# Stick-breaking attention on one core: five softplus chains issued two banks deep, and the weighted values issued at the end of the next pair's period

## The chip, the cores and the metric

One core of a Trainium2 chip runs the whole kernel in one launch. The metric is device microseconds (us) of that core. The engines spoken of are TensorE (PE: matrix products into PSUM, which has eight banks here), VectorE (DVE), ScalarE (ACT), GpSimd (POOL) and SyncE (SP, which issues the loads of the weights).

## What is computed

Two transformer blocks on one sequence of 512 tokens, 1024 wide, in float32. The change lies in the attention of the second block: sixteen heads of 64, each query weighs earlier keys by a stick that is broken key by key.

```python
def stick_breaking_attention(xn, w_qkv, q_gain, k_gain, w_o):
    qkv = (xn @ w_qkv).reshape(b, s, 3, SB_HEADS, SB_HEAD_DIM)
    q = rms_norm(qkv[:, :, 0], q_gain)       # k likewise; v plain
    ...
    z = einsum('bhqd,bhkd->bhqk', q, k) * scale
    mask = s_idx < t_idx
    log_beta = log_sigmoid(z)
    log_1m = where(mask, log_sigmoid(-z), 0.0)
    rev = cumsum(log_1m, axis=3, reverse=True)
    rev_excl = concatenate([rev[..., 1:], 0])
    w = where(mask, exp(log_beta + rev_excl), 0.0)
    outs.append(einsum('bhqk,bhkd->bhqd', w, v))
    ...
    return o @ w_o
```

With sp = softplus(z) the weight is exp(z - sp - sum of sp over the keys between), which is how the kernel forms it.

## The kernel before

**The whole.** Four feed-forward parts, a first mixer and this attention follow each other. Nearly all products are made of three matmuls each (`mm3`, lines 180 to 182): weights and activations are split into a high part, rounded to fp32r by ACT (line 157 for a weight, line 175 for an activation), and the rest, made by DVE (lines 158 and 176).

**The attention stage.** A generator, `sb_dense`, issues the projections that make Q, K and V: `qk_tile` for two heads' Q or K, `sv_tile` for a quarter of V, then part of the output projection. A second one, `stick`, issues the attention of one pair of heads after the other, eight pairs, 0 to 7. `Flow` (F) lets them take turns: after each `yield n` of `stick`, n steps of `sb_dense` are issued (`F.pull(n)`). One step is three matmuls of 512 columns, or six of 256 in `sv_tile`. `F.at(d, f)` runs f when d more steps have been issued. So a Q or K tile's norm follows its projection: `first` scales it (line 759) and squares it on ACT (line 761), and seven steps on `second` sums the squares with one matmul (line 766, into a bank `pm`), takes the inverse root on ACT (lines 209, 210) and DVE (lines 212 to 214), and scales the tile (line 769).

**One pair.** `front` (lines 833 to 842) takes five PSUM banks, A1, A0, Z2, B1 and B0, and fills them with the scores of the two heads: head A lies in A0, A1 and half of Z2, head B in B0, B1 and the other half. `soft` makes softplus of a bank in place of four operations, each on 128x512: magnitude on DVE (line 850), exponential and logarithm on ACT (lines 851, 852), and on DVE the sum with max(z, 0) (line 853). `split` makes high and low parts of the result (lines 175 and 176). `middle(.., g)` subtracts the running sums with matmuls into the same banks (lines 865 to 871): g = 0 is head A, which needs the softplus of A1, A0, Z2 and the splits of these three in that order, g = 1 is head B. `weights` takes the exponential of a bank (line 874), which is its last use. `back` (lines 878 to 885) multiplies the weights of a pair with V into a bank `po`, and splits that.

**What sets the order.** PE, ACT and SP execute in the order in which the code issues. DVE and POOL are put into an order by a scheduler when the program is built, and that order is fixed from then on. Buffers come from pools: eight banks of PSUM (`bank`), 66 slots of 128x512 (`sl`).

In the code before, a bank's four softplus operations are issued together, and the `back` of the pair before stands in the midst of the pair's period, ahead of `middle`.

Of the kernel before, what the change touches and what calls it, by code (L numbers as in the profile page):

```python
# [10 lines left out]
I32 = mybir.dt.int32  # L11
F32R = mybir.dt.float32r
AF = mybir.ActivationFunctionType
OP = mybir.AluOpType
# [60 lines left out]
def block_kernel(ctx: ExitStack, tc: tile.TileContext, a, out):  # L75
    nc = tc.nc
    dve, act, pe, pool = nc.vector, nc.scalar, nc.tensor, nc.gpsimd
# [9 lines left out]
    def sl(dt=F32):  # L87
        return slots.tile([P, S], dt, name="sl", tag="sl")

    def bank():  # L90
        return psum.tile([P, S], F32, name="ps", tag="ps")
# [236 lines left out]
    F = Flow()  # L328
# [421 lines left out]
    def qk_tile(n, which, g):  # L750
        ps = bank()
        yield from proj(ps, a["sb_qk"][n], 1024, zs)
        if "r2" not in state:
            state["r2"] = nx.rstd()
            F.at(7, lambda: column_of(state["r2"], rcol2))

        def first():
            t = sl()
            dve.tensor_tensor(t, ps, state["r2"], op=OP.mult)
            sq = sl()  # L760
            act.activation(sq, t, AF.Square)
            F.at(NORM_LAG, lambda: second(t, sq))

        def second(t, sq):
            pm = bank()
            pe.matmul(pm, halves, sq, start=True, stop=True)  # L766
            rs = sl()
            rsqrt(rs, pm, 1.0 / 64)
            dve.scalar_tensor_tensor(t, t, g, rs, op0=OP.mult, op1=OP.mult)
            if which is K:  # L770
                pool.tensor_copy(kz[n % 3][HALF[1], :], t[HALF[1], 2 * P:3 * P])
            F.at(SCALE_LAG, lambda: which.__setitem__(n % 8, t))
        F.at(1, first)
# [48 lines left out]
    def stick():  # L822
# [19 lines left out]
                    pe.matmul(z[b][:, c:c + P], ident_r, hidden_r, start=False, stop=True, skip_group_check=True)  # L842
            return z

        def soft(z):

            def one(b):
                t = sl()

                dve.tensor_scalar(t.bitcast(I32), z[b].bitcast(I32), 0x7FFFFFFF, None, op0=OP.bitwise_and)  # L850
                act.activation(t, t, AF.Exp, scale=-1.0)  # L851
                act.activation(t, t, AF.Ln, bias=1.0)  # L852
                dve.scalar_tensor_tensor(t, z[b], 0.0, t, op0=OP.max, op1=OP.add)  # L853
                return t
            return one

        def middle(z, sp, hl, g):
            for j in ((3, 1, 0, 2), (3, 1, 2, 0))[g]:
# [30 lines left out]
        for n in range(KD):  # L889
            while n not in K and F.pull(1):  # L890
                pass
            while n not in K:
                F.t += 1
                F.fire()
            z = front(n)
            one = soft(z)
            sp, hl = {}, {}
            sp[A1] = one(A1)
            yield 2
            sp[A0] = one(A0)  # L900
            yield 2
            hl[A1] = split(sp[A1])
            sp[Z2] = one(Z2)
            yield 2
            hl[A0] = split(sp[A0])
            sp[B1] = one(B1)
            yield 3
            hl[Z2] = split(sp[Z2])
            if n:
                while v[1][(n - 1) // 2] is None and F.pull(1):  # L910
                    pass
                back(n - 1, last)
            yield 2
            sp[B0] = one(B0)
            hl[B1] = split(sp[B1])
            middle(z, sp, hl, 0)
            yield 1
            hl[B0] = split(sp[B0])
            yield 3
            weights(z, sp, A1)  # L920
            weights(z, sp, A0)
            middle(z, sp, hl, 1)
            for b in (B1, Z2, B0):
                weights(z, sp, b)
            yield 5
            last = sp
        yield 7
        back(KD - 1, last)
# [1 line left out]
    F.dense = sb_dense()  # L930
    for steps in stick():
        F.pull(steps)
    while F.pull(1):
        pass
    F.settle()

    norm = Norm()
# [127 lines left out]
```

## Time and profile before

| | us |
|---|---|
| median of three runs | 2193.16 |
| lowest, highest | 2192.76, 2193.18 |
| the profiled execution | 2191.18 |
| its span (first to last instruction) | 2189.4 |
| attention stage, from the scores of pair 0 to the end of the values of pair 7 | 1509 to 1795 |
| DVE and ACT busy, share of the span | 50%, 38% |

The profile is of one execution. An engine's busy time is the time in which it executes something. "Idle before" in brackets is how long an engine stood still ahead of an instruction, with the engine, tile and line that released it. PEclk is the granted TensorE clock as a share of 2.4 GHz; 0.50 is 1.2 GHz. In a row of the timeline that stands for several matmuls, the duration is that of the whole row.

### The profile page before, as it was taken

What the parts mean: (1) busy time and instruction counts of PE and PEld (TensorE: products, weight loads), DVE (VectorE), ACT (ScalarE), POOL (GpSimd) and SP (SyncE); (2) the same over time, 40 slices, a digit from 0 to 9 for tenths busy, and PEclk for the clock granted to TensorE, in tenths of its full rate; (3) what the DMA queues carried; (4) which work ended last, traced back from release to release, by engine and by line L of the source; (5) the groups of instructions that cost most, each with busy time, mean ns of one, the idle gap of its engine ahead of it and who ended that gap; (6) DMA issues with size and microseconds to landing.
All of it is one profiled execution on the core that took longest, in us unless ns stands there. A gap on an engine that the chain in (4) does not pass through costs nothing.

```text
span 2189.4 us, 24877 instructions
## 1 busy us (share of the span) xinstructions
PE 2126.0 (97%) x10038; PEld 1747.2 (80%) x10038; DVE 1097.2 (50%) x1600; ACT 829.7 (38%) x1287; POOL 24.2 (1%) x50
## 2 busy tenths in 40 slices
PE   8999999999999999999999999998988899999999
PEld 6888888887888788888888888886766678888887
DVE  6444334799945644444454444346555646444332
ACT  5222222376766432222233222224454445222211
POOL 0000000000002000000000000000000000000000
PEclk9999999999999999999999999999999999999999
DMA  4332334222212333333323233331111113323341
GB/s 163 112 96 97 89 97 118 88 91 71 78 44 79 109 97 96 97 97 91 102 79 114 97 97 93 101 101 62 48 35 43 39 37 117 97 97 96 93 122 54
DMA packets 57267, 193.43 MB, mean 88 GB/s; under 512 B 6784, under 2 KB 6784, under 8 KB 57152
## 3 DMA queue, kind: packets, MB, share of 16 engines
q1 hardware_dynamic: 55296, 188.28, 27.3%
q0 software_dynamic: 640, 2.10, 0.3%
q8 instruction: 78, 1.28, 0.2%
q10 hardware_dynamic: 1216, 1.47, 0.2%
q14 instruction: 37, 0.30, 0.0%
HBM read 189.07 MB, written 2.10 MB: 87 GB/s over the span
## 4 chain that ended last, share of the span: by engine, by line
PE 80%; issue 9%; DVE 8%; ACT 3%; DMA 0%; POOL 0%; SPq 0%; DVEq 0%; POOLq 0%
PE ps L180 25%; PE ps L181 24%; PE ps L182 24%; DVE wl L158 1%; PE ps L883 1%; DVE sl L176 1%; ACT sl L851 1%; ACT sl L852 1%; PE ps L871 1%; DVE sl L495 1%; PE ps L870 1%; DVE sl L850 1%; PE ps L865 1%; DVE m L493 1%; PE ps L766 0%
## 5 line engine op out<-in xcount | busy, mean ns | idle before, releaser
L180 PE MATMUL ps<-sl,wh 128*128 128x512 f32 x2704 | 1069.3, 395 | 10.0 <-ACT sl L247 6.5
L181 PE MATMUL ps<-sl,wh 128*128 128x512 f32 x2704 | 1057.0, 391 | 2.4 <-DVE sl L248 1.6
L182 PE MATMUL ps<-sl,wl 128*128 128x512 f32 x2704 | 1056.0, 391 | 0.0
L180 PEld LDWEIGHTS ps<-sl,wh 128*128 128x128 f32 x2704 | 509.7, 189 | 120.5 <-issue 6.8
L181 PEld LDWEIGHTS ps<-sl,wh 128*128 128x128 f32 x2704 | 510.1, 189 | 109.2 <-issue 2.9
L182 PEld LDWEIGHTS ps<-sl,wl 128*128 128x128 f32 x2704 | 509.8, 189 | 107.3
L158 DVE TENSOR_TENSOR wl<-wraw,wh 128x1024 fp32r<-128x1024 f32 (+3 forms) x368 | 434.8, 1183 | 313.4 <-ACT wh L157 312.9
L157 ACT ACTIVATE wh<-wraw 128x1024 fp32r<-128x1024 f32 (+3 forms) x368 | 373.0, 1015 | 514.4 <-issue 238.0
L175 ACT ACTIVATE sl<-sl 128x512 fp32r<-128x512 f32 x145 | 91.0, 627 | 394.6 <-DVE sl L277 383.2
L277 DVE TENSOR_TENSOR sl<-ps,sl 128x512 f32<-128x512 f32 x88 | 60.9, 692 | 265.9 <-PE ps L182 259.9
L176 DVE TENSOR_TENSOR sl<-sl 128x512 fp32r<-128x512 f32 x145 | 101.7, 701 | 72.0 <-ACT sl L175 71.0
L275 DVE TENSOR_TENSOR sl<-ps,sl 128x512 f32<-128x512 f32 x88 | 60.8, 691 | 138.5 <-PE ps L182 138.3
L228 ACT ACTIVATE sl<-x 128x512 f32<-128x512 f32 x42 | 25.8, 627 | 123.6 <-DVE x L297 97.4
L296 DVE SCALAR_TENSOR_TENSOR sl<-ps,sl 128x512 f32<-128x512 f32 x32 | 22.1, 692 | 79.7 <-PE ps L182 79.7
L276 ACT ACTIVATE sl<-sl 128x512 f32<-128x512 f32 x88 | 54.1, 615 | 12.2 <-DVE sl L275 12.2
L883 PE MATMUL ps<-sl 128*64 128x512 f32 (+3 forms) x128 | 25.8, 551 | 32.1 <-DVE sl L213 20.5
L514 ACT ACTIVATE sl<-sl,mx 128x128 f32<-128x128 f32 (+3 forms) x64 | 35.7, 558 | 41.1 <-DVE mx L513 41.0
L851 ACT ACTIVATE sl<-sl 128x512 f32<-128x512 f32 x40 | 25.1, 628 | 66.7 <-DVE sl L850 66.7
L883 PEld LDWEIGHTS ps<-sl 128*64 128x64 f32 x128 | 10.0, 168 | 48.3 <-DVE sl L213 21.6
L853 DVE SCALAR_TENSOR_TENSOR sl<-ps,sl 128x512 f32<-128x512 f32 x40 | 27.7, 692 | 40.9 <-ACT sl L852 40.9
L521 ACT ACTIVATE sl<-sl,sm 128x128 f32<-128x128 f32 (+3 forms) x64 | 35.9, 560 | 25.3 <-DVE sm L520 14.6
L597 PE MATMUL ps<-sl 128*128 128x256 f32 (+2 forms) x176 | 43.2, 327 | 0.8 <-DVE mx L513 0.8
(136 smaller groups left out, 1333.9 us busy)
## 6 DMA issues: line engine op xcount, KB each, us to landing
wraw<-in_f_in_dram SPq DMA_DIRECT2D x176, 512.0 KB
wraw<-in_f_out_dram SPq DMA_DIRECT2D x64, 512.0 KB
wraw<-in_mix_t_dram SPq DMA_DIRECT2D x34, 512.0 KB
wraw<-in_f_out_dram SPq DMA_DIRECT2D x32, 384.0 KB
wraw<-in_sb_qk_dram SPq DMA_DIRECT2D x16, 512.0 KB
wraw<-in_br_dram SPq DMA_DIRECT2D x16, 256.0 KB
wraw<-in_w_out_dram SPq DMA_DIRECT2D x8, 512.0 KB
wraw<-in_sb_v_dram SPq DMA_DIRECT2D x8, 512.0 KB
```

The lines of the kernel that those rows point to most:

```text
L157: act.activation(wh[:, :n], raw[:, :n], AF.Copy)
L158: dve.tensor_tensor(wl[:, :n], raw[:, :n], wh[:, :n].bitcast(F32), op=OP.subtract)
L175: act.activation(h, x, AF.Copy)
L176: dve.tensor_tensor(l, x, h.bitcast(F32), op=OP.subtract)
L180: pe.matmul(ps, wh, xh, start=start, stop=False)
L181: pe.matmul(ps, wh, xl, start=False, stop=False)
L182: pe.matmul(ps, wl, xh, start=False, stop=stop)
L275: dve.tensor_tensor(g, pg, rs, op=OP.mult)
L276: act.activation(g, g, AF.Silu)
L277: dve.tensor_tensor(g, pu, g, op=OP.mult)
L851: act.activation(t, t, AF.Exp, scale=-1.0)
L883: pe.matmul(po[HALF[g], sb * P:], v[sb // 2][n // 2][:, cv:cv + 64], t[b][:, c:c + S - sb * P], start=sb == 0, stop=sb == 3)
```

## The change

The four softplus operations become three functions, and a loop of six turns issues them shifted against each other: in one turn the magnitude of the bank after next, the exponential and logarithm of this bank, the sum of the bank before, and the split of the bank before that. Each of the first four turns is followed by three steps of projections, the other two by one. `middle` of head A then comes after fourteen steps; the split of B1 is issued behind it. `back` of the pair before goes from ahead of `middle` to behind the weights of the present pair, and ahead of it further steps are issued until six have passed since the last norm matmul (`bank_free`) and until the V tile is there. Two steps then stand between `back` and the next pair's scores. At the end the rest of `sb_dense` is issued until it is exhausted. No operation is added or removed, and the loads are the same.

```diff
         def second(t, sq):
             pm = bank()
+            state["bank_free"] = F.t + 6
...
             z = front(n)
-            one = soft(z)
             sp, hl = {}, {}
-            sp[A1] = one(A1)
-            yield 2
-            sp[A0] = one(A0)
-            yield 2
-            hl[A1] = split(sp[A1])
-            sp[Z2] = one(Z2)
-            yield 2
-            hl[A0] = split(sp[A0])
-            sp[B1] = one(B1)
-            yield 3
-            hl[Z2] = split(sp[Z2])
-            if n:
-                while v[1][(n - 1) // 2] is None and F.pull(1):
-                    pass
-                back(n - 1, last)
-            yield 2
-            sp[B0] = one(B0)
+            order = (A1, A0, Z2, B1, B0)
+            for t in range(6):
+
+                for b in order[:2] if t == 0 else order[t + 1:t + 2]:
+                    sp[b] = absolute(z, b)
+                if t < 5:
+                    log_part(sp[order[t]])
+                if 1 <= t:
+                    soft(sp[order[t - 1]], z[order[t - 1]])
+                if 2 <= t < 5:
+                    hl[order[t - 2]] = split(sp[order[t - 2]])
+                yield 3 if t < 4 else 1
+            middle(z, sp, hl, 0)
             hl[B1] = split(sp[B1])
-            middle(z, sp, hl, 0)
             yield 1
             hl[B0] = split(sp[B0])
             yield 3
...
             for b in (B1, Z2, B0):
                 weights(z, sp, b)
-            yield 5
+            yield 1
+            if n:
+                while F.t < state["bank_free"] and F.pull(1):
+                    pass
+                while v[1][(n - 1) // 2] is None and F.pull(1):
+                    pass
+                back(n - 1, last)
+            yield 2
             last = sp
...
-    while F.pull(1):
-        pass
+    while F.dense is not None:
+        F.pull(1)
```

The three places below are all in the period of pair 4. Lines of the changed kernel are a little higher: the norm matmul is 767, the magnitude 849, exponential and logarithm 853 and 854, the sum 858, `middle` 868 to 874, the weights 877, `back` 886.

On PE before, from the norm matmul of a K tile into its bank ps_12401 on; ps_12427 is the bank `po` of pair 3:

```order
L766 MATMUL ps_12401<-sl_12351,cmat_102 128x512
L180 MATMUL ps_12413<-sl_10382,wh_12170 128x512
L181 MATMUL ps_12413<-sl_10383,wh_12170 128x512
L182 MATMUL ps_12413<-sl_10382,wl_12171 128x512
L883 MATMUL ps_12427<-sl_12063,sl_12108 64x512
L883 MATMUL ps_12427<-sl_12214,sl_12108 64x512
L883 MATMUL ps_12427<-sl_12046,sl_12108 64x384
```

On PE now, from the norm matmul of that tile on; ps_12265 to ps_12268 are banks of pair 4:

```order
L767 MATMUL ps_12434<-sl_12375,cmat_102 128x512
L180 MATMUL ps_12446<-sl_10382,wh_12195 128x512
L181 MATMUL ps_12446<-sl_10383,wh_12195 128x512
L182 MATMUL ps_12446<-sl_10382,wl_12196 128x512
L868 MATMUL ps_12267<-sl_12325,nlater_11064 128x128
L868 MATMUL ps_12266<-sl_12325,nones_11066 128x128
L868 MATMUL ps_12267<-sl_12325,nones_11066 128x128
L868 MATMUL ps_12268<-sl_12325,nones_11066 128x128
L873 MATMUL ps_12267<-sl_12413,nlater_r_11068 128x384
```

Before, one step and then `back` followed the norm matmul; now one step and then `middle` of head B does, and `back` comes after five more steps.

On ACT before, from the split of A1 on; sl_12338, 12356, 12371, 12386 and 12446 are the softplus tiles of A1, A0, Z2, B1 and B0, and sl_12419 is a projected tile on the way to its norm:

```order
L175 ACTIVATE sl_12367<-sl_12338 128x512
L851 ACTIVATE sl_12371<-sl_12371 128x512
L852 ACTIVATE sl_12371<-sl_12371 128x512
L175 ACTIVATE sl_12382<-sl_12356 128x512
L851 ACTIVATE sl_12386<-sl_12386 128x512
L852 ACTIVATE sl_12386<-sl_12386 128x512
L157 ACTIVATE wh_12397<-wraw_12175 128x1024
L209 ACTIVATE sl_12404<-ps_12401,epst_105 128x512
L210 ACTIVATE sl_12404<-sl_12404 128x512
L761 ACTIVATE sl_12421<-sl_12419 128x512
L175 ACTIVATE sl_12423<-sl_12371 128x512
L175 ACTIVATE sl_12436<-ps_12427 128x512
```

On ACT now, from the split of A1 on; the softplus tiles of A1, A0, Z2, B1 and B0 are sl_12285, 12287, 12311, 12325 and 12358, and the tile on the way to its norm is sl_12373:

```order
L175 ACTIVATE sl_12330<-sl_12285 128x512
L157 ACTIVATE wh_12343<-wraw_11994 128x1024
L209 ACTIVATE sl_12350<-ps_12347,epst_105 128x512
L210 ACTIVATE sl_12350<-sl_12350 128x512
L853 ACTIVATE sl_12325<-sl_12325 128x512
L854 ACTIVATE sl_12325<-sl_12325 128x512
L175 ACTIVATE sl_12363<-sl_12287 128x512
L761 ACTIVATE sl_12375<-sl_12373 128x512
L853 ACTIVATE sl_12358<-sl_12358 128x512
L854 ACTIVATE sl_12358<-sl_12358 128x512
L175 ACTIVATE sl_12386<-sl_12311 128x512
L175 ACTIVATE sl_12413<-sl_12325 128x512
```

Before, the splits of A1 and A0 stood ahead of the norm's lines 209 and 210 and that of Z2 behind the square (line 761). Now only that of A1 stands ahead of them, and the exponential and logarithm of B0 as well as the split of Z2 stand behind the square.

On DVE before, from the low part of A0 on (sl_12407 is the norm's tile):

```order
L176 TENSOR_TENSOR sl_12383<-sl_12356,sl_12382 128x512
L850 TENSOR_SCALAR sl_12386<-ps_12320 128x512
L853 SCALAR_TENSOR_TENSOR sl_12386<-ps_12320,sl_12386 128x512
L158 TENSOR_TENSOR wl_12398<-wraw_12175,wh_12397 128x1024
L212 SCALAR_TENSOR_TENSOR sl_12407<-sl_12404 128x512
L213 SCALAR_TENSOR_TENSOR sl_12407<-ps_12401,sl_12407 128x512
L214 SCALAR_TENSOR_TENSOR sl_12403<-sl_12407,sl_12404 128x512
```

On DVE now, from line 213 of the norm on (sl_12353 is the norm's tile, sl_12364 the low part of A0):

```order
L213 SCALAR_TENSOR_TENSOR sl_12353<-ps_12347,sl_12353 128x512
L858 SCALAR_TENSOR_TENSOR sl_12325<-ps_12267,sl_12325 128x512
L214 SCALAR_TENSOR_TENSOR sl_12349<-sl_12353,sl_12350 128x512
L849 TENSOR_SCALAR sl_12358<-ps_12268 128x512
L770 SCALAR_TENSOR_TENSOR sl_12304<-sl_12304,qg_180,sl_12349 128x512
L176 TENSOR_TENSOR sl_12364<-sl_12287,sl_12363 128x512
L759 TENSOR_TENSOR sl_12373<-ps_12298,sl_11106 128x512
L858 SCALAR_TENSOR_TENSOR sl_12358<-ps_12268,sl_12358 128x512
L176 TENSOR_TENSOR sl_12387<-sl_12311,sl_12386 128x512
```

Before, the low part of A0 was made ahead of the norm; now it stands five places behind line 213, and line 759, whose result the square reads, stands right behind it.

## Rows read from the trace of the kernel before

**Rows 1.** The page's first part: busy time of TensorE, share, instructions.
```profile
PE 2126.0 (97%) x10038; PEld 1747.2 (80%) x10038; DVE 1097.2 (50%) x1600; ACT 829.7 (38%) x1287; POOL 24.2 (1%) x50
```

**Rows 2.** Waits of PE in the attention stage (1505 to 1800 us).
```profile
PE ps L883 <- DVE sl L213: 20.5, 3, 7.2
PE ps L883 <- DVE sl L746: 11.6, 3, 4.4
PE ps L870 <- ACT sl L175: 5.7, 1, 5.7
PE ps L865 <- DVE sl L853: 1.7, 1, 1.7
PE ps L871 <- DVE sl L176: 0.4, 1, 0.4
```

**Rows 3.** Timeline of PE: `back` of pair 1 and of pair 6 (start, us).
```profile
1599.63 3.90 PE L883 MATMUL ps<-sl 128*64 128x512 f32 x16 [7.25 <-DVE sl L213]
...
1775.93 2.38 PE L883 MATMUL ps<-sl 128*64 128x512 f32 x16
```

**Rows 4.** Busy time and clock by stretch: stretch, length, PE, PEld, DVE, ACT, POOL, PEclk, DMA.
```profile
1529.20:1535.00 5.80, 5.66 (x17) 4.54 (x18) 4.09 (x6) 3.36 (x5) 0.00 (x0) 0.55 0.00 0
...
1748.70:1753.00 4.30, 4.26 (x16) 1.71 (x16) 2.74 (x5) 0.00 (x0) 0.29 (x1) 0.51 0.00 0
1780.00:1786.00 6.00, 3.88 (x25) 3.15 (x24) 4.18 (x7) 4.06 (x8) 0.00 (x0) 1.00 0.01 3
```

**Rows 5.** Timeline of ACT and DVE in pair 2: softplus of bank Z2, then B1's exponential.
```profile
1591.40 0.63 ACT L851 ACTIVATE sl<-sl 128x512 f32<-128x512 f32 x1 [1.44 <-DVE sl L850]
1592.06 0.63 ACT L852 ACTIVATE sl<-sl 128x512 f32<-128x512 f32 x1
1592.60 0.61 ACT L175 ACTIVATE sl<-sl 128x512 fp32r<-128x512 f32 x1
1592.73 0.69 DVE L853 SCALAR_TENSOR_TENSOR sl<-ps,sl 128x512 f32<-128x512 f32 x1 [1.36 <-ACT sl L852]
1593.33 0.68 DVE L176 TENSOR_TENSOR sl<-sl 128x512 fp32r<-128x512 f32 x1
...
1594.65 0.63 ACT L851 ACTIVATE sl<-sl 128x512 f32<-128x512 f32 x1 [1.44 <-DVE sl L850]
```

**Rows 6.** The same timeline a little later: the norm of a K tile.
```profile
1596.79 0.67 ACT L209 ACTIVATE sl<-ps,epst 128x512 f32<-128x512 f32 x1
1597.49 0.63 ACT L210 ACTIVATE sl<-sl 128x512 f32<-128x512 f32 x1
...
1598.88 0.69 DVE L213 SCALAR_TENSOR_TENSOR sl<-ps,sl 128x512 f32<-128x512 f32 x1
...
1600.29 0.69 DVE L759 TENSOR_TENSOR sl<-ps,sl 128x512 f32<-128x512 f32 x1
...
1601.01 0.63 ACT L761 ACTIVATE sl<-sl 128x512 f32<-128x512 f32 x1 [2.88 <-DVE sl L759]
1601.54 0.61 ACT L175 ACTIVATE sl<-sl 128x512 fp32r<-128x512 f32 x1
```

**Rows 7.** Timeline of PE: step, norm matmul, `middle` (1536.31 to 1539.08); scores (1581.39 to 1585.12).
```profile
1534.75 0.40 PE L180 MATMUL ps<-sl,wh 128*128 128x512 f32 x1
...
1535.45 1.02 PE L766 MATMUL ps<-sl,cmat 128*128 128x512 f32 x2
1536.31 0.38 PE L865 MATMUL ps<-sl,nlater 128*128 128x128 f32 x2
...
1539.08 0.28 PE L735 MATMUL ps<-wh,sl 128*128 128x256 f32 x1
...
1581.39 2.42 PE L833 MATMUL ps<-sl 64*128 64x384 f32 x14
...
1585.12 0.45 PE L180 MATMUL ps<-sl,wh 128*128 128x512 f32 x1
```

**Rows 8.** Busy time of each engine, summed over the eight pairs (1509.1 to 1800).
```profile
sum 290.90, PE 250.87 PEld 197.52 DVE 160.40 ACT 140.88 POOL 2.04; mean PE 31.36 PEld 24.69 DVE 20.05 ACT 17.61 POOL 0.26
```

More of the change, by code (lines that the diff above doesn't have):

```diff
@@ L843, in front, with absolute, log_part, soft @@
             return z
[L845 to L855, printed above, removed]
+        def absolute(z, b):
+            t = sl()
+            dve.tensor_scalar(t.bitcast(I32), z[b].bitcast(I32), 0x7FFFFFFF, None, op0=OP.bitwise_and)
+            return t
+        def log_part(t):
+            act.activation(t, t, AF.Exp, scale=-1.0)
+            act.activation(t, t, AF.Ln, bias=1.0)
+        def soft(t, z):
+            dve.scalar_tensor_tensor(t, z, 0.0, t, op0=OP.max, op1=OP.add)
         def middle(z, sp, hl, g):
```

## The prediction, made before the changed kernel ran

> **What bounds the kernel now.** I read the page's busy shares first: PE is busy 97% of the span [rows 1], so outside the attention stage nothing is to be had from other engines' order, and the change touches nothing there. Next, PE's waits inside the stage: 39.9 us in nine waits [rows 2]. 32.1 us are `back`: three times it waits for line 213, three times for line 746. One wait of 5.7 us is `middle` of pair 0, and 2.1 us lie in pair 7. Then the timeline at such a wait: `back` of pair 1 stands still for 7.25 us, because its bank is the one that a norm matmul has just filled and line 213 is that bank's last reader; line 213 stands in DVE's queue behind the whole softplus of four banks. The row also shows a second cost: this `back` takes 3.90 us, that of pair 6, with no wait ahead, 2.38 us [rows 3]. So I looked at the granted clock last. Behind each of the seven long waits (3.6 us and more) there is a stretch of 3.4 to 5.8 us in which PE works on and the mean clock is 0.51 to 0.59; behind the wait of 1.7 us it stays at 1.00 [rows 4] (the first and the last of the seven, and that one). Busy time times what is missing from 1.00 gives 5.66 x 0.45 = 2.6 us for the first, 4.26 x 0.49 = 2.1 us for the last, and 1.7, 1.6, 1.6, 1.6 and 1.7 us between: 12.9 us. What can be won is thus 39.9 + 12.9 = 52.8 us. DVE and ACT are busy 160 and 141 of the stage's 291 us [rows 8]; both have room, so it is order, not work, that makes PE wait.
>
> **The softplus chain.** Before, a bank costs 3.25 us from exponential to next exponential (1591.40 to 1594.65): exponential, logarithm, sum, low part and next magnitude follow each other across ACT and DVE, and each engine waits 1.4 us for the other in every bank [rows 5]. Issued shifted, ACT has about 0.66 + 0.54 + 0.6 = 1.8 us a bank and DVE three operations at 0.6 to 0.7, about 2 us, with neither waiting for the other. Over the three banks that run one by one this takes about 3 x 1.25 = 3.7 us from the chain of a pair. No operation is added, and all of this lies beside PE's work as long as `middle` comes late enough.
>
> **`back` moved.** Its matmuls cost the same wherever they stand, 2.4 us a pair at full clock [rows 3], and so do the split's two operations and the steps issued with it. Behind the weights it asks, in the new order, twice for line 746 and once for line 213, each time with `middle` of head B or five steps of cover in between, and otherwise for banks released long before. I take its waits of 32.1 us as gone. Who is behind it: the scores of the next pair, which need the five weights' exponentials. From the end of `middle` of head B to the scores stand three steps and `back`, 3 x 0.70 + 2.4 = 4.5 us, before five steps, 3.5 us; three exponentials at about 0.6 us are done in 1.8 us. So that costs nothing, and it would begin to cost if ACT were 2.7 us late there. SP's loads are unmoved: they hang on the projections, of which the same number is issued. The tiles of the old pair's weights live longer; no row shows what that costs, and I take nothing, with 0 to 2 us for the range, since 66 slots hold them.
>
> **What is late next: `middle`.** What `back` waited for was partly the chain that `middle` needs as well. I walk the worst pair, 4, in the new order, from the start of its scores. PE: scores 3.7 us, nine steps of 0.70, norm matmul 0.86, five steps: `middle` of head A begins at 14.4 [rows 7]. It takes 2.8 us unhindered; shared out by columns it asks for A0's parts 1.6 and 1.8 us after its start, for those of Z2 at 2.1 and 2.2. ACT: line 209 comes 0.2 us behind the norm matmul, at 11.05. Line 213 is 2.1 us behind line 209, at 13.1 [rows 6]. On DVE four operations at 0.65 us stand between it and A0's low part, which is made 16.4 to 17.1; line 759 follows to 17.7. The square waits for that, then come exponential and logarithm of B0 (0.53, 0.65, 0.55 us) and the high part of Z2, done at 20.05; its low part at 20.9. So PE waits 17.1 - 16.2 = 0.9 us for A0, 20.05 - 17.35 = 2.7 us for Z2's high part, 0.75 us for its low part: 4.3 us. It is the square that stands in ACT's queue ahead of the softplus; the rows show it doing so, 2.88 us idle, with the split of Z2, whose input was there 7 us earlier, right behind it [rows 5, 6].
>
> Walked in the same way: pair 0, 2.5 us in four waits below 0.8 us; pair 1, 3.1 us (Z2's split is behind a weight's high part and B0's exponential); pair 2, 1.3 us in head A and 1.8 us in head B, where its second norm stands ahead of B1's split; pairs 3 and 5, 1.9 us each; pair 6 as pair 4, 4.3 us; pair 7 none. Together 2.5 + 3.1 + 3.1 + 1.9 + 4.3 + 1.9 + 4.3 = 21.1 us.
>
> The walk's hand-overs come from rows in which the engines were less full; a third either way, 7 us, goes into the range.
>
> **The clock.** None of the new waits reaches 3.6 us; most are below 1.2 us. The waits of 2.7 us in pairs 4 and 6, with 0.9 us ahead and little work between, lie between the row that lost the clock and the one that kept it. I count both as losing it, at 1.7 us (the middle of the seven), 3.4 us. Ends: 0 and all seven, 12.9 us.
>
> **Sum.** Waits 39.9 - 21.1 = 18.8 us less, clock 12.9 - 3.4 = 9.5 us less: 28.3 us. The profiled execution took 2191.18 us (span 2189.4), so 2162.9; the median of the runs is 1.98 us above that execution, so about 2165.
>
> The Trainium skill (Perfetto Trace Analysis, Optimization Strategy) says that the same gap repeating on the engine that should be full can mean that there is too little PSUM for the next tile. The 7.25 us gaps of `back` fit this, the three waits for line 746 don't: those wait for V itself. By that rule alone the gain would be the bank's 20.5 us and the clock behind those three, 1.6 + 1.6 + 2.1 us, 25.8 us, and 2167 us, with `middle` as it was.
>
> **Rivals.**
> 1. *The waits go, the clock doesn't come back.* If several waits below 3 us, close together, drop the clock as one long one does, each pair keeps its loss: gain 18.8 us, 2174. For it: in pairs 1 and 3 to 6 PE does only a few short matmuls in the 3 to 5 us around the waits. Against: the stretch with waits of 0.4 and 1.7 us at 1.00 [rows 4]. Chance 0.22.
> 2. *The wait only moves.* `middle` waits for everything `back` waited for, as the norm's chain is unchanged. Then only the one-by-one chain's 3.7 us of a pair would count where nothing else ends later, and that can be eaten by the longer way to the split of Z2: 2190 to 2195. Against: DVE is busy only 55% of the stage [rows 8], and between norm and `middle` lie more steps now. Chance 0.06.
> 3. *Slower: norms ahead of the splits.* If in ACT's queue a whole norm comes in front of the parts that `middle` asks for, from line 209 to the square and behind it, 4.2 + 0.5 = 4.7 us [rows 6], and ACT is so late that nothing of it is covered, `middle` waits 4.7 us more than walked and the clock goes with it, 1.7: 6.4 us a pair. Four pairs cost 25.6 us and leave a little of the 28.3; from the fifth on the kernel is slower than before, and with all seven it is 2165 + 45 = 2210. The order has a square ahead of Z2's split in pairs 2, 4 and 6, which the walk has counted; it would take ACT some 4 us later than walked in the other pairs too. Chance 0.04.
> 4. *The walk is too dark*: some tenths each way empty the small waits, 5 us of the 21, and no clock is lost: 28.3 + 5 + 3.4 = 36.7 us gained, 2156.5. Chance 0.08.
>
> My forecast has the remaining 0.60.
>
> **How the numbers follow.** Forecast 2165. The range reaches down to 28.3 + 3.4 + 7 = 38.7 us gained, 2154.5, and up past rival 1 with the walk a third too short: 18.8 - 7 = 11.8 us gained, 2181. Outside lie rivals 2 and 3 and a little of the rest. Within 0.2%, 4.4 us, a measurement can't tell the two apart; faster by more holds the forecast and rivals 1 and 4, 0.60 + 0.22 + 0.08 = 0.90; same is rival 2, 0.06; slower rival 3, 0.04.
>
> **What would show it.** Right: no wait of `back` for line 213 or 746 above 1 us; waits of `middle` (now lines 868 to 874) on lines 175 and 176 of about 20 us in some fifteen pieces, the longest 2.7 us in pairs 4 and 6 on line 175; clock 1.00 in most of the stage. The scores of pair 7 start near 1734 us instead of 1766.6. Wrong: a wait of `middle` above 3.5 us, a wait of the scores for the weights' exponentials, a clock at 0.5 in most pairs, or PE waiting for weights (line 157 or 158).

## The result, and the profile after

The changed kernel's median is 2167.49 us (2164.55 to 2168.47) beside 2193.17 us of the kernel before: ratio 0.988, 95% interval 0.9863 to 0.9898, 25.7 us faster. The profiled execution took 2167.2 us, its span 2165.4 us. The forecast was 2165.0 us and the range 2154.5 to 2181.

The page's first part, busy time of each engine, answers to [rows 1]:

```profile
PE 2127.4 (98%) x10038; PEld 1750.7 (81%) x10038; DVE 1094.6 (51%) x1600; ACT 828.0 (38%) x1287; POOL 24.4 (1%) x50
```

The waits of PE in the attention stage (1505 to 1820 us; engine, line, who was waited for: sum, times, longest) answer to [rows 2]:

```profile
PE ps L873 <- ACT sl L175: 9.9, 9, 2.5
PE ps L874 <- DVE sl L176: 6.2, 12, 0.8
```

Nine waits of 39.9 us have become twenty-one of 16.1 us, all of them `middle`'s for the splits. `back` waits nowhere, and in pairs 0 to 5, taken singly, it takes 2.37 to 2.38 us as in the undisturbed row of [rows 3]. The stage, from the scores of pair 0 to the first addition of the output projection, was 291.9 us long and is 267.1: 24.8 us less, and what lies around it has kept its length (2189.4 - 291.9 = 1897.5; 2165.4 - 267.1 = 1898.3).

The stretches behind `middle`'s waits, as in [rows 4] (stretch, length, busy time of PE, PEld, DVE, ACT, POOL, granted clock, DMA share, GB/s), in pairs 0, 1, 3, 4, 5 and 6:

```profile
1529.40:1534.00 4.60, 4.60 (x21) 3.59 (x21) 1.32 (x2) 1.23 (x3) 0.00 (x0) 0.69 0.41 114
1559.60:1564.00 4.40, 4.35 (x15) 3.72 (x16) 3.11 (x4) 2.61 (x5) 0.00 (x0) 0.62 0.22 86
...
1624.10:1628.00 3.90, 3.89 (x16) 3.56 (x17) 3.17 (x5) 1.92 (x4) 0.00 (x0) 0.56 0.65 194
1657.90:1663.00 5.10, 5.07 (x17) 3.96 (x17) 2.40 (x3) 1.17 (x2) 0.00 (x0) 0.67 0.27 103
1693.00:1699.00 6.00, 4.92 (x30) 4.34 (x31) 4.54 (x8) 3.28 (x6) 0.00 (x0) 1.00 0.57 171
1726.80:1732.00 5.20, 5.19 (x26) 4.73 (x26) 1.16 (x2) 0.20 (x1) 0.00 (x0) 0.67 0.00 0
```

Five of the six are low. Busy time by what is missing from 1.00 is 1.4 + 1.7 + 1.7 + 1.7 + 1.7 = 8.2 us.

The longest wait, in pair 4, on PE (start, duration, engine, line, what, and in brackets the idle time ahead):

```profile
1654.17 0.50 PE L874 MATMUL ps<-sl,nlater_r 128*128 128x512 f32 x1 [0.73 <-DVE sl L176]
...
1657.13 0.38 PE L873 MATMUL ps<-sl,nlater_r 128*128 128x256 f32 x1 [2.46 <-ACT sl L175]
```

and on DVE and ACT ahead of it:

```profile
1654.03 0.68 DVE L759 TENSOR_TENSOR sl<-ps,sl 128x512 f32<-128x512 f32 x1
...
1654.75 0.63 ACT L761 ACTIVATE sl<-sl 128x512 f32<-128x512 f32 x1 [3.44 <-DVE sl L759]
1655.28 0.61 ACT L853 ACTIVATE sl<-sl 128x512 f32<-128x512 f32 x1
1655.93 0.63 ACT L854 ACTIVATE sl<-sl 128x512 f32<-128x512 f32 x1
1656.46 1.65 ACT L175 ACTIVATE sl<-sl 128x512 fp32r<-128x512 f32 x3
```

This is the row that the prediction walked: the square stands still 3.44 us for line 759, B0's exponential and logarithm come behind it, and Z2's split, for which PE waits, last.

### The profile page after: what moved, and what is told of

It is laid out like the page before. It is cut to its first block, busy times and chain, and to the rows that moved or that the text cites. A ratio compares the mean times of both kernels' runs of the same rounds, so it can differ in the third digit from the quotient of the medians.

```text
span 2165.4 us, 24870 instructions
## 1 busy us (share of the span) xinstructions
PE 2127.4 (98%) x10038; PEld 1750.7 (81%) x10038; DVE 1094.6 (51%) x1600; ACT 828.0 (38%) x1287; POOL 24.4 (1%) x50
## 4 chain that ended last, share of the span: by engine, by line
PE 81%; issue 9%; DVE 7%; ACT 3%; DMA 0%; POOL 0%; ACTq 0%; DVEq 0%; POOLq 0%
PE ps L180 25%; PE ps L181 25%; PE ps L182 25%; DVE wl L158 1%; PE ps L886 1%; PE ps L834 1%; DVE sl L495 1%; PE ps L874 1%; DVE m L493 1%; PE ps L767 0%; PE ps L873 0%; DVE sl L176 0%; PE ps L735 0%; PE ps L413 0%; PE ps L412 0%
## 5 line engine op out<-in xcount | busy, mean ns | idle before, releaser
L296 DVE SCALAR_TENSOR_TENSOR sl<-ps,sl 128x512 f32<-128x512 f32 x32 | 22.1, 692 | 79.7 <-PE ps L182 79.7
L276 ACT ACTIVATE sl<-sl 128x512 f32<-128x512 f32 x88 | 54.2, 616 | 12.2 <-DVE sl L275 12.2
L229 DVE TENSOR_TENSOR sl<-sl 128x512 f32<-128x512 f32 x49 | 33.4, 692 | 20.9 <-ACT sl L228 20.4
L735 PE MATMUL ps<-wh,sl 128*128 128x256 f32 x128 | 40.4, 316 | 0.0
L212 DVE SCALAR_TENSOR_TENSOR sl<-sl 128x512 f32<-128x512 f32 x23 | 15.9, 693 | 47.8 <-ACT sl L210 47.7
L597 PEld LDWEIGHTS ps<-sl 128*128 128x128 f32 x176 | 33.0, 189 | 8.5 <-DVE mx L513 1.2
```

The costliest lines, as they stand in the source:

```text
L276: act.activation(g, g, AF.Silu)
L597: pe.matmul(ps[:, :n], q[:, i * P:(i + 1) * P], part[:, :n], start=x_ == 0, stop=x_ == 1)
L735: pe.matmul(dst, hh, wh[:, cl], start=kk == 0 and b == 0, stop=False)
```

## All runs in one table

"Waits" are PE's waits in the stage; "clock" is the busy time of PE times what is missing from a granted clock of 1.00, summed over slices of 4 us of the stage (by this sum the changed kernel has 7.5 us, not the 8.2 of the hand-picked stretches; where the slices begin moves a sum by up to 0.3 us); "stage" is its length. Waits, clock and stage are those of the profiled execution, the median is that of all runs. All in us; the ratio is to the kernel before on the same chip.

| kernel | median | ratio, 95% interval | waits | clock | stage |
|---|---|---|---|---|---|
| before | 2193.17 | | 39.9 | 12.3 | 291.9 |
| changed | 2167.49 | 0.988 (0.9863 to 0.9898) | 16.1 | 7.5 | 267.1 |
| e1_back_only | 2192.43 | 0.9999 (0.999 to 1.0009) | 32.0 | 16.4 | 291.9 |
| e2_pipe_only | 2152.88 | 0.9816 (0.9801 to 0.9831) | 8.4 | 3.1 | 252.3 |
| e3_no_gate | 2168.51 | 0.9885 (0.9871 to 0.99) | 16.1 | 7.4 | 267.2 |
| e4_square_pool | 2164.99 | 0.9867 (0.9851 to 0.9884) | 12.8 | 4.4 | 260.1 |
| e5_back_ahead | 2161.59 | 0.9856 (0.9839 to 0.9872) | 14.0 | 7.9 | 261.2 |
| e6_steps_ahead | 2166.77 | 0.9884 (0.9869 to 0.9899) | 19.4 | 8.5 | 266.8 |
| e7_fill | 2161.22 | 0.9859 (0.9844 to 0.9873) | 8.6, rest filled | 1.5 | 260.9 |
| e8_best | 2165.60 | 0.9878 (0.9863 to 0.9893) | 16.3 | 6.8 | 262.4 |
| e9_back_later | 2144.32 | 0.9778 (0.9763 to 0.9792) | 2.8 | 1.4 | 244.1 |
| e10_fill_ends | 2143.82 | 0.978 (0.9763 to 0.9796) | 0.8, rest filled | 0.0 | 243.4 |
| e11_gate_place | 2154.30 | 0.9827 (0.9812 to 0.9842) | 8.9 | 3.0 | 254.7 |

From before to e9 waits and clock fall by 37.1 + 10.9 = 48.0 us and the stage by 47.8: between these two kernels they account for the stage's length. For the changed kernel they fall by 28.6, the stage by 24.8.

## Experiments: one half of the change at a time

The change has two halves, the pipeline and the move of `back`. Each was run alone. The halves are not pure: both runs have the 14 steps ahead of head A's `middle`, where before there were 11, and the new loop at the end.

**e1_back_only**: the move, with each bank's softplus in one go.

```diff
-            for t in range(6):
-                ...
-                yield 3 if t < 4 else 1
+            def one(b):
+                sp[b] = absolute(z, b)
+                log_part(sp[b])
+                soft(sp[b], z[b])
+            one(A1)
+            yield 3
+            one(A0)
+            yield 3
+            hl[A1] = split(sp[A1])
...
```

> The changed kernel with the weighted values at the end of the next pair's period, but each bank's softplus issued in one go as before (absolute value, Exp, Ln, closing step), in the same 14 steps of projections. My theory (both parts are needed): the back's waits of 32.1 us [rows 2] stay gone, but the five serial chains of 3.25 us each end some 3 us later than the pipelined ones, so each of the eight middles waits about 3 us more on the splits and the clock falls there; 2180 to 2190 us. Rival (the move of the weighted values is all of the gain): no longer waits in the middle than in the changed kernel, within 3 us of 2167.

**e2_pipe_only**: the pipeline, with `back` and its loop for the V tile where they stood before.

```diff
                 yield 3 if t < 4 else 1
+                if t == 2 and n:
+                    while v[1][(n - 1) // 2] is None and F.pull(1):
+                        pass
+                    back(n - 1, last)
...
-            if n:
-                while F.t < state["bank_free"] and F.pull(1):
-                    pass
-                while v[1][(n - 1) // 2] is None and F.pull(1):
-                    pass
-                back(n - 1, last)
```

> The changed kernel's software pipeline, but the weighted values issued where they stood before, behind the third turn of the next pair's softplus. My theory: back waits again, in seven of eight pairs, mostly for the norm chain's line 213 (product and reciprocal root) that holds the PSUM banks, some 15 to 25 us of waits in all, and the clock is low behind them; 2178 to 2190 us. Rival (the pipeline alone is the gain): back waits less than 5 us in all, within 3 us of 2167.

The waits of PE in the stage, e1 first:

```profile
PE ps L873 <- ACT sl L175: 15.3, 8, 3.1
PE ps L868 <- DVE sl L858: 9.6, 4, 3.7
PE ps L874 <- DVE sl L176: 7.1, 9, 1.6
```

and e2:

```profile
PE ps L886 <- DVE sl L213: 5.0, 3, 1.8
PE ps L873 <- ACT sl L175: 1.9, 4, 0.6
PE ps L874 <- DVE sl L176: 1.5, 4, 0.4
```

In e1 `back` waits no more, and `middle` waits 32.0 us in its place. With 16.4 us of lost clock nothing is won: alone, the move is worth 0.7 us by the medians, which the interval can't tell from nothing. I had expected 2180 to 2190. In e2, which I expected to lose against the changed kernel, 40.3 us are won. **The whole gain is the pipeline's, and on top of it the move costs 2167.5 - 2152.9 = 14.6 us.** My theory that both were needed had fallen. What the three additional steps have of e2's 40.3 us was not measured alone; the shifted order is worth 2192.4 - 2167.5 = 24.9 us between e1 and the changed kernel, which have the same steps (only the split of B1 stands elsewhere in e1, ahead of `middle`).

Why the pipeline alone frees `back`: its bank is released by line 213, and what made that late was not the norm but the queue ahead of it. The timeline of PE before, at the norm matmul of the K tile whose bank the `back` of 7.25 us waits for (line 209 behind it is the first row of [rows 6]):

```profile
1590.66 1.02 PE L766 MATMUL ps<-sl,cmat 128*128 128x512 f32 x2
```

and PE, ACT and DVE in e2, in the same pair:

```profile
1580.97 1.02 PE L767 MATMUL ps<-sl,cmat 128*128 128x512 f32 x2
...
1582.29 0.67 ACT L209 ACTIVATE sl<-ps,epst 128x512 f32<-128x512 f32 x1
...
1584.38 0.69 DVE L213 SCALAR_TENSOR_TENSOR sl<-ps,sl 128x512 f32<-128x512 f32 x1
1585.12 2.37 PE L886 MATMUL ps<-sl 128*64 128x512 f32 x16 [1.76 <-DVE sl L213]
```

Before, line 209 started 1596.79 - 1590.66 = 6.1 us behind its matmul, since two banks' softplus, with a hand-over in each, stood ahead of it in ACT's queue; in e2 it is 1.3 us. From line 209 to line 213 both take 2.09 us. `back` stood one step behind the norm matmul and waited 7.25 us; in e2 it stands two behind and waits 1.76.

With line 746, V's evacuation, it is the same. The last matmul of a V tile in pair 1 and the evacuation of its second half, before and then in e2:

```profile
1555.15 0.28 PE L737 MATMUL ps<-wh,sl 128*128 128x256 f32 x1
...
1564.34 0.87 DVE L746 TENSOR_SCALAR sl<-ps,rcol 128x256 f32<-128x256 f32 x2
```

```profile
1551.32 0.28 PE L737 MATMUL ps<-wh,sl 128*128 128x256 f32 x1
...
1555.92 0.87 DVE L746 TENSOR_SCALAR sl<-ps,rcol 128x256 f32<-128x256 f32 x2
```

Before, 9.2 us lie between the two, and DVE stood idle for 1.36 us twice in between, each time for ACT's logarithm; in e2 it is 4.6 us.

## Experiments: what the move costs, and why

Three things could make the moved `back` cost 14.6 us: the added loop on `bank_free`, the 2.4 us of PE work that no longer stand ahead of `middle`, and the steps that its loop for the V tile issues. The Q, K and V tiles of two pairs take 48 steps; the yields of two pairs issue 42. The others are issued by whichever loop first asks for a tile that isn't there. In e2 this is the V loop ahead of `back`, in the softplus of pairs 1, 3 and 5, so that 20 steps in place of 14 stand ahead of `middle` there (before it was the same loop, 18 or 19 steps in place of 11). In the changed kernel no pair has more than 14, and the others fall behind the second `middle`, where the softplus has no use for them: in pairs 4 and 6 eight steps stand there in place of three.

**e3_no_gate**: the loop on `bank_free` taken out.

```diff
             if n:
-                while F.t < state["bank_free"] and F.pull(1):
-                    pass
                 while v[1][(n - 1) // 2] is None and F.pull(1):
```

> The changed kernel without the loop that holds the weighted values back until six steps after a norm's PSUM bank was taken; nothing else changes. My theory: by the end of the period line 213 has long read the norm's bank, so back finds a bank without the gate too; within 2 us of 2167.5, no wait of back. Rival (the gate is what removes back's wait): back waits 1 us or more for line 213 in several pairs; 2172 to 2180 us.

The same waits to the tenth, and 2168.5 us: this loop is neither needed nor harmful.

**e11_gate_place**: e3 with the V loop, and nothing else, back behind the third turn; `back` stays at the end.

```diff
                 yield 3 if t < 4 else 1
+                if t == 2 and n:
+                    while v[1][(n - 1) // 2] is None and F.pull(1):
+                        pass
...
             if n:
-                while v[1][(n - 1) // 2] is None and F.pull(1):
-                    pass
                 back(n - 1, last)
```

> e2_pipe_only with nothing moved but the weighted values, to the end of the next pair's period as in the changed kernel; the loop that waits for the value tile stays behind the third turn, so the projection steps, norms and their places are those of e2_pipe_only (20 steps ahead of the middle in pairs 1, 3 and 5, 14 in the others). Theory A (what costs the changed kernel 14.6 us against e2_pipe_only is where the six extra steps of every two pairs and the norms fall): the middle's waits in pairs 1 to 6 stay under 4 us in all, and only pair 7, which has six steps left ahead of its middle, waits some 3 us more; 2151 to 2158 us. Theory B (the back's own 2.4 us of cover are what is missed): waits of about 1.5 to 2.4 us in each of the pairs 2, 4 and 6 and low clocks behind them; 2161 to 2168 us.

```profile
PE ps L874 <- DVE sl L176: 4.9, 12, 0.7
PE ps L873 <- ACT sl L175: 3.7, 8, 0.7
PE ps L868 <- DVE sl L858: 0.3, 1, 0.3
```

The two lines of the loop are worth 2168.5 - 2154.3 = 14.2 us by the medians, and 12.5 us of stage. By its time theory A held. Its sign held only in part: `middle` waits 5.9 us in pairs 1 to 6, not under 4, and 1.6, 1.6 and 1.4 us of that lie in pairs 2, 4 and 6, which theory B had named. So the cover is real. Between these two places of `back` it comes out even, 1.4 us between e11 and e2, since e2 has three waits of `back`, 5.0 us, in place of these; a third place is tried in e9 below. What the steps do is seen in the order on PE. Pairs 1, 3 and 5 have 20 steps ahead of `middle` in e11 and 14 in e3; and in pairs 4 and 6 the norm matmul stands behind the seventh of the 14 steps in e11, behind the ninth in e3, so that the norm is through two steps earlier there, and `middle` waits 1.6 and 1.4 us in place of 3.6 and 3.5.

**e5_back_ahead** and **e6_steps_ahead** asked whether cover alone explains it: `back` and the V loop right ahead of `middle`, and `back` at the end with three more steps ahead of `middle`.

```diff
# e5
+            if n:
+                while v[1][(n - 1) // 2] is None and F.pull(1):
+                    pass
+                back(n - 1, last)
             middle(z, sp, hl, 0)
# e6
-                yield 3 if t < 4 else 1
+                yield 4 if t < 3 else 3 if t < 4 else 1
...
-            yield 1
             if n:
...
-            yield 2
             last = sp
```

> The changed kernel with the weighted values right ahead of head A's middle, behind all 14 steps of the softplus, in place of the end of the period. My theory after e2_pipe_only (back is 2.4 us of TensorE work that needs nothing of its own pair's softplus; ahead of the middle it covers the softplus, behind the middle it covers nothing that anyone waits for): the middle's waits of pairs 1 to 7, 14.5 us in the changed kernel, vanish all but 2 us, the norms are through by then, so the three waits of back in e2_pipe_only, 5.0 us, vanish too; only pair 0's 1.6 us and the clock loss behind them stay; 2143 to 2149 us. Rival (behind the third turn is the right place for another reason, for instance that the split of its result comes early): 2152 us or more.

> The changed kernel with the weighted values at the end of the period as they are, but three of the seven projection steps behind the first middle moved ahead of it, to 17 from 14. My theory (cover): three steps by .70 us are 2.1 us, nearly the 2.4 us of a back, so the middle's waits fall from 16.1 to under 6 us and the clock stays up in most pairs; 2150 to 2157 us. Rival (the place of back itself decides, by its PSUM bank or its split): waits above 12 us, 2163 to 2168 us; or the waits move to the scores, which find no cover behind the last weights: 2160 or more.

Both fell: the times lie where the rivals had put them, but the reasons are others than theirs. In e5 `middle` waits only in pair 0, as expected, but `back` waits again, as in [rows 2] and [rows 3]:

```profile
PE ps L886 <- DVE sl L213: 11.5, 3, 4.3
PE ps L886 <- DVE sl L746: 0.9, 1, 0.9
```

In pair 1 the V loop finds only one step to issue there (15 ahead of `middle`, where e2 has 20), so that from then on the projections run five steps behind those of e2, and the norms stand elsewhere: in pairs 2, 4 and 6 a second norm matmul comes two steps ahead of `back`, and behind it ACT has the rest of two banks' softplus, two splits and a weight's high part to do before line 209 (in pair 2 norm matmul 1581.74, line 209 at 1585.55, line 213 at 1587.71).

In e6 three steps more ahead of `middle` did not shorten its waits (19.4 us in all). In pairs 2 and 4 a second norm matmul now stands four steps ahead of `middle`, and from line 209 to the square this norm is in ACT's queue ahead of Z2's split, as the prediction's third rival feared. In pair 4:

```profile
1658.55 0.67 ACT L209 ACTIVATE sl<-ps,epst 128x512 f32<-128x512 f32 x1
...
1662.69 0.63 ACT L761 ACTIVATE sl<-sl 128x512 f32<-128x512 f32 x1 [2.81 <-DVE sl L759]
...
1665.08 0.39 PE L873 MATMUL ps<-sl,nlater_r 128*128 128x256 f32 x1 [4.53 <-ACT sl L175]
```

Even in pairs 3 and 5 `middle` waits 0.74 and 0.75 us for Z2's high part, as in the changed kernel, 0.75 and 0.74. In pair 3 the magnitude of B0 starts 1620.44 - 1605.21 = 15.2 us behind the scores in the changed kernel and 1629.17 - 1612.09 = 17.1 us in e6. The turns are issued between the steps, and the steps bring work of their own into the same two queues: V's evacuation (line 746) and the split of the weights (lines 157, 158) stand there ahead of it. So in this pair 1.9 us of delay came with 2.1 us of steps. As the norm matmul moved too (in pair 3 from behind the seventh step to behind the second), the two can't be told apart here. By these rows, steps give cover only where what they bring into ACT's and DVE's queues does not come between the softplus and `middle`.

## Experiments: the clock, and the square

**e7_fill**: the changed kernel with useless matmuls in the waits ahead of Z2 in pairs 1, 3, 4, 5 and 6 (32 in all, 7.4 us of them at .23 us, which run while PE would wait).

```diff
+    FILL = {1: 6, 3: 3, 4: 10, 5: 3, 6: 10}
...
+                if j == 2 and g == 0:
+                    for _ in range(fill):
+                        pe.matmul(z[A1], zeros_r, hl[A1][0], start=False, stop=True, skip_group_check=True)
```

> The changed kernel with useless matmuls (a zero weight, 128x512, .23 us each, added into a score bank) in TensorE's row ahead of the Z2 part of head A's middle: 6 in pair 1, 3 in pairs 3 and 5, 10 in pairs 4 and 6. They fill waits and add work only where a wait is shorter. My theory (the low clock behind the middle is caused by the waits ahead of it): the waits in pairs 1, 4 and 6 shrink to under 1 us and the granted clock behind them is 1.00, where it was .62 to .67 for some 5 us; 4 to 6 us faster than the changed kernel, 2161 to 2164 us. Rival (the clock falls for another reason): clock as low as before in the same places, 2167 to 2170 us.

The same stretches in pairs 0 (not filled), 1, 3, 4 and 6:

```profile
1529.20:1534.00 4.80, 4.80 (x20) 3.87 (x21) 1.75 (x2) 1.50 (x3) 0.00 (x0) 0.68 0.36 105
1559.50:1564.00 4.50, 4.21 (x24) 3.72 (x25) 3.92 (x6) 2.86 (x5) 0.00 (x0) 1.00 0.26 100
...
1622.70:1627.00 4.30, 4.24 (x27) 3.87 (x28) 3.13 (x6) 1.88 (x4) 0.00 (x0) 1.00 0.61 208
1655.00:1660.00 5.00, 4.94 (x25) 3.95 (x26) 2.44 (x4) 2.28 (x4) 0.00 (x0) 1.00 0.30 97
...
1722.30:1727.50 5.20, 5.12 (x38) 4.64 (x39) 1.23 (x3) 1.45 (x3) 0.00 (x0) 1.00 0.02 3
```

Every filled pair is at 2.4 GHz, the one left alone is not, and the kernel is 6.3 us faster than the changed one (its runs lie at 2160.95 to 2161.47), as much as the clock sum fell (7.5 - 1.5 = 6.0). So the low clock comes from the short waits ahead of it. The Trainium skill (TensorE: Matmul & The Clock Gate, A second HAM failure mode: psum-queue depth-cycling) has a case of this kind, in which short idle times between groups of matmuls, coming often, pull the clock down again and again; the rows here agree, with waits of 0.4 to 2.5 us in the four pairs that had lost the clock and were filled.

**e4_square_pool**: the square of line 761 on GpSimd.

```diff
-            act.activation(sq, t, AF.Square)
+            pool.tensor_tensor(sq, t, t, op=OP.mult)
```

> The changed kernel with the square of each projected tile (line 761) on GpSimd in place of ScalarE. My theory: the longest waits of the middle, 2.46 and 2.47 us in pairs 4 and 6, come from a square that stands in ScalarE's queue ahead of Exp and split and waits for VectorE's product; without it both fall under 1 us and the clock stays up behind them; 2159 to 2164 us. Rival (the waits come from VectorE's own queue, so taking the square off changes nothing): waits of 2 us or more stay in both pairs, 2165 to 2170 us; slower, if GpSimd's square makes the norm late.

```profile
PE ps L874 <- DVE sl L176: 8.5, 11, 1.6
PE ps L873 <- ACT sl L175: 3.5, 4, 1.4
PE ps L767 <- POOL sl L761: 3.4, 3, 1.3
```

The waits of 2.46 and 2.47 us for Z2's high part are gone, so the square made them; waits of 1.30 us for its low part have come in their place, since DVE was as late; I had expected both under 1 us, and the time is just outside the expected range. The stage is 7.0 us shorter, the kernel only 2.5 us, less than the intervals tell apart: on GpSimd a square takes 1.36 us in the median where ACT takes 0.63, and the norms ahead of the first scores, which have little cover, wait for it (1.33 and 1.29 us, the last two; these 2.6 of the 3.4 us lie ahead of the stage); the scores of pair 0 start at 1515.64 in place of 1510.03. The wait moved out of the stage to its door.

## A version that is faster than both

**e9_back_later**: e2 with `back` one turn later; the V loop stays, so that every step keeps its place.

```diff
                 if t == 2 and n:
                     while v[1][(n - 1) // 2] is None and F.pull(1):
                         pass
-                    back(n - 1, last)
+                if t == 3 and n:
+                    back(n - 1, last)
```

> e2_pipe_only with the weighted values one turn later, behind the fourth turn; the loop that waits for the value tile stays behind the third, so each pair keeps the number of projection steps that it has there and every norm its place. My theory (back's three waits for line 213 in e2_pipe_only, 1.8, 1.8 and 1.5 us, are there because it comes two steps behind the norm's matmul): three steps more are 2.1 us, so these waits vanish, 5.0 us, and the middle still waits only in pairs 0 and 7; 2146 to 2150 us. Rival (the split of back's result, a turn later in ScalarE's and VectorE's rows, now makes the middle wait): 2152 us or more, waits of the middle in pairs 2, 4 and 6.

```profile
PE ps L874 <- DVE sl L176: 1.9, 5, 0.4
PE ps L873 <- ACT sl L175: 0.9, 2, 0.5
```

2144.3 us, 48.5 us under before and 23.2 us under the changed kernel: no wait of `back`, seven of `middle`, none above 0.5 us, and one low stretch left, pair 0's. That is below the expected 2146 to 2150. The steps and the V loop are alike in e2, e9 and e11; only the place of `back` differs, and the times are 2152.9, 2144.3 and 2154.3 us. So the place is worth up to 10.0 us: here neither `back` nor `middle` has to wait long.

**e10_fill_ends** puts useless matmuls into the waits of pairs 0 and 7.

```diff
+            def keep():
+                for _ in range(fill):
+                    pe.matmul(z[A1], zeros_r, hl[A1][0], start=False, stop=True, skip_group_check=True)
...
-            middle(z, sp, hl, 0)
+            middle(z, sp, hl, 0, 2 if n in (0, 7) else 0)
```

> e9_back_later with useless matmuls (zero weight, 128x512, .23 us each) in the four waits of the middle in pairs 0 and 7, two in each. My theory (waits of .3 to .6 us in a row lower the clock, and work in them keeps it up): the granted clock behind these two middles, .67 and .79 in e2_pipe_only, stays at 1.00 and 2 to 3 us are won; 2143 to 2148 us. Rival (so short waits don't matter and the clock falls there for another reason): no gain over e9_back_later, or up to 2 us slower for the added work.

Pair 0 became 29.7 - 28.3 = 1.4 us shorter, and its clock stays at 1.00. Pair 7, which in e9 had one wait of 0.41 us and no low clock any more, became 0.7 us longer. The medians differ by 0.5 us, which can't be told from nothing; 2 to 3 us were expected. **e8_best** was an attempt from e5: three more steps in pair 0, and `back` of pair 6 behind the first turn of pair 7.

> e5_back_ahead with two edits for the ends of the row of pairs: pair 0, which has no back to cover its softplus, gets three more steps ahead of its middle, and in pair 7 the weighted values of pair 6 come behind the first turn, so that the output projection's steps that need them can run earlier. My theory: no wait in the middle above .5 us and no low clock in the stage; 2140 to 2147 us, 2 to 4 us under e5_back_ahead. Rival (the steps taken early are missing at the end): within 1 us of e5_back_ahead or slower.

It is 4.0 us slower than e5 by the medians, but not all of that need be the edits' price: of the 3.0 us between the two profiled executions 1.8 us lie ahead of the scores of pair 0, where the code is the same, and 1.3 us in the stage. Nothing was won: pair 0 itself waits 2.38 and 1.17 us now, and the three waits of e5 for line 213 are still there (11.3 us). The two edits were not run apart.

## Why the prediction was right, and where it was wrong

The time came within 2.5 us. Its parts did not come so close.

- **Back's waits gone**: right, all 32.1 us, and no other line waits for lines 213 or 746.
- **Middle's waits, 21.1 us**: 16.1 measured, and in every pair less than walked: 1.6 for 2.5 in pair 0, 2.2 for 3.1, 1.1 and 1.1 for 1.3 and 1.8 in pair 2, 1.4 for 1.9 in pairs 3 and 5, 3.6 and 3.5 for 4.3, none in pair 7. Places, one cause (the square, e4) and proportions were right; the sum was a quarter too long. In pair 4 the three waits were 0.73, 2.46 and 0.42 us for the walked 0.9, 2.7 and 0.75; which hand-over of the walk was too long was not taken apart. There were twenty-one pieces, not fifteen.
- **The clock, 3.4 us**: mis-sized. Five stretches lost it, not two, 7.5 to 8.2 us. The step that failed is that only waits that approach 3.6 us count; pair 3 lost it by two waits of 0.75 and 0.70 us. Rival 1's condition held in five pairs; its price, the whole 12.9 us, did not come.
- **The sum**: waits 5.0 us too dark, clock 4.1 to 4.8 us too bright. That the two errors took each other out is luck; the forecast was nearer than its reasons. Waits and clock together should have shortened the stage by 28.6 us, and it was 24.8. A part of the rest may lie in the number of waits: a matmul of 512 columns takes .39 us and follows the last one after .23, so that each stop costs some .16 us which counts as busy, 1.9 us for twelve stops more. This is worked out, not tested, and it gives half of the 3.8 us. The table fits it: this rest (the fall of waits and clock less the fall of the stage) is 3.1 to 4.0 us in the five kernels with sixteen waits or more (changed, e1, e3, e4, e11) and at most 1.1 us in e2, e5, e6, e8 and e9, with seven to thirteen. What the other half is stays open.
- **The wrong step.** The prediction said of the moved `back` that its matmuls, its split and "the steps issued with it" cost the same wherever they stand. For matmuls and split that is nearly so between e2 and e11 (1.4 us), but not in general: e9 is 10.0 us faster than e11 by the place of `back` alone. For the steps it is wrong by 14.2 us (e3 and e11). The prediction also gave the move the credit for `back`'s waits; e2 shows that the pipeline takes 27.1 of the 32.1 us away without it, and e1 that the move alone turns them into waits of `middle`. Rival 2, priced at 2190 to 2195, is what e1 is, at 2192.4.
- **The scores of pair 7** start at 1743.79, not near 1734: the whole gain up to there is 22.8 us, and I had put more than the final gain ahead of that point.
- By the rule of the Trainium skill (Perfetto Trace Analysis, Optimization Strategy) the sum would have been 2167 us, which is the median. Its reason isn't borne out: the waits for line 746 went with the others, and e9 has no wait of `back` at all with as many banks as before. The repeating gap went without a bank more, as soon as the bank's reader was no longer late in its queue; what a further bank would have done was not tried.

## What to carry to other kernels

When an instruction is moved, ask what its guard does: a loop that issues other work until an input is there moves that work too, and here this was worth 14.2 us, more than the place of the instruction itself (1.4 to 10.0 us). Operations that pass between two in-order engines are best issued shifted against each other, since what suffers from a chain issued in one go is also the short work queued behind it, here a norm's. And before two halves of a change are kept together, run each alone.

## What the runs showed of the hardware

Which short waits lower the clock I can't say. In e11 the same row of four waits stands in pair 0 (.46, .30, .41, .42 us) and in pair 2 (.52, .31, .40, .42 us), and again in pair 4 (.46, .30, .40, .42 us); the stretches behind them, and behind two waits of .74 and .70 us in pair 6:

```profile
1530.40:1535.00 4.60, 4.60 (x18) 3.56 (x19) 1.59 (x2) 1.15 (x3) 0.00 (x0) 0.65 0.30 105
...
1593.20:1598.00 4.80, 4.75 (x32) 4.14 (x33) 2.70 (x4) 2.51 (x4) 0.00 (x0) 1.00 0.30 100
...
1657.20:1662.00 4.80, 4.80 (x32) 4.18 (x33) 2.69 (x4) 2.42 (x4) 0.00 (x0) 1.00 0.35 113
...
1721.00:1726.00 5.00, 4.89 (x20) 4.38 (x21) 4.50 (x7) 2.99 (x5) 0.00 (x0) 0.66 0.64 207
```

The changed kernel's pair 5 has the waits of this pair 6, .74 and .70 us, and stayed at 1.00; its pair 3, with .75 and .70 us, fell to 0.56. And in e2 one wait of 1.76 us, ahead of `back` in pair 2, left the clock at 1.00:

```profile
1585.00:1590.00 5.00, 4.88 (x27) 3.19 (x28) 3.85 (x8) 3.06 (x6) 0.29 (x1) 1.00 0.28 104
```

So the length of the waits alone doesn't decide, and a low stretch can't be forecast from it; what e7 shows is that with the longest of them filled there was none in those pairs.
